# Output stage, roots and last attention sums of a hybrid attention and state-space layer, on one core

## The chip, the cores and the metric

One Trainium2 chip, one of its cores. The metric is the device time of one execution in microseconds (us), the median of several runs. One further execution was profiled; all rows below come from that one. Engines: PE is TensorE (PEld its weight loads), DVE is VectorE, ACT is ScalarE, POOL is GpSimd, SP is SyncE, whose queue issues nearly all DMAs.

## The reference, cut to what matters

One layer over 2176 tokens (128 of a prompt, 2048 latent ones), width 1024. `h = rms_norm(x) * scale + shift` is projected; one half of the result feeds differential attention (8 heads, two softmax maps each), the other a bidirectional state-space scan. Both halves are normalised, gated and projected back:

```python
a   = softmax(q1 k1) - lam * softmax(q2 k2);  att = a @ v          # per head
att = rms_norm(att, subln_g) * (1 - lam_init) * silu(g_att)
y   = rms_norm((y_f + y_b + D_skip * xs) * silu(z), ssd_norm_g)
out = concatenate([att, y]) @ w_out
y_out = rms_norm(x + gate * out, final_g)
# rms_norm(x, g) = x * rsqrt(mean(x*x) + 1e-6) * g
```

## The kernel before

The tokens are cut into 17 chunks of 128, the prompt being chunk 0. Every float32 operand of the large matmuls is split into a high part (a copy rounded by ACT) and a low part (the difference, by DVE), and each product is three matmuls: high by high, high by low, low by high.

**Order.** The program is not written in the order in which it is issued. Every operation is recorded first with its engine, a cost from a small table of formulas (`price`, line 289) and its dependences, buffer reuse included. A backward pass (`latest`, line 345) gives each operation a due time, with TensorE's work kept in program order; then a list scheduler (`simulate`, line 366) lets each engine take, among what is ready by these costs, the operation with the earliest due time. That gives one fixed order for each engine and for SP's queue; on the chip each engine runs its order and waits where an input is late. All instructions are emitted by one helper, so the profile gives line 232 for nearly all of them, and they are told apart by the names of their tiles.

**Stages.** Projections and the scan fill the first 1500 us. From about 1475 to 1550 us lie the last projection units, the inputs of the first two output chunks (`load_y`, line 1305, called for chunks 0 and 1 at line 1362 with a pool of its own, `pey`, whose ring `yr` has three buffers) and the prompt's small attention. Attention over the latent tokens follows (about 1557 to 2806 us): 128 units (8 heads, 16 query chunks), two units to a pair. For unit i, `frame(i)` (line 1583) scores six groups of 768 keys, three for each of two softmax maps, into PSUM (`ps_s`); DVE copies each out (tile `S`) with its running maximum; `s_max` (1490) takes the maximum of three; `s_exp` (1495) exponentiates a whole map of 2304 keys on ACT; `combine` (1500) forms the first map minus lambda times the second on POOL; `t_high` (1511) transposes the result on TensorE (`ps_t`), two frames later in program order, and ACT and DVE make its high and low parts (`aH`, `aL`); `av` multiplies by the values (`ps_o`). Sums of squares over each pair's output are one small matmul (`ps_q`, in `av_ssq`, 1563), whose row goes to memory and comes back in `rms_rows` (1670), with a transpose (`ps_r`), a root and a reciprocal, to be broadcast in `load_a`.

**Output stage** (about 2787 us to the end). For each chunk c, 96 matmuls of 512 columns: eight blocks of `w_out` for the y half first, then eight for the attention half. Chunks 0 and 1 run their y half together while attention drains. `load_y(c + 1)` is issued half-way through chunk c: three loads (`ya` from `y_d`, `yx` from `xbc_d`, `yz` from `z_d`), elementwise work in place in the single buffer `ya`, a sum of squares (`ysq`, `ysm`), a matmul that sums it over partitions (`ps_n`), root and reciprocal, and the parts `yH`, `yL`, which have two buffers each. `load_a(c)` (1685) does the same for the attention half with the single buffers `raw`, `rb`, `ga`, `a0`, `a1`. `finish_out` (1748) applies gate, residual and the last norm and stores. The weights `w_out` pass through the ring `yr` of pool `p3a` (three buffers, then used by `load_y`) and, for the last eight, through the ring `o` (three buffers). PSUM for output chunks comes from two pools: `psF0`, opened when the scores are done, and `psF1`, opened when attention's `psT` and `psO` close.

Of the kernel before, what the change touches and what calls it, by code (L numbers as in the profile page):

```python
# [9 lines left out]
F32 = mybir.dt.float32  # L10
# [19 lines left out]
EPS = 1e-6  # L30
TINY = 1e-37
# [10 lines left out]
B_YR, B_O = 3, 3  # L42
# [400 lines left out]
def body(tc, I, O):  # L443
# [30 lines left out]
    eps_t = cp.tile([P, 1], F32, name="eps_t")  # L474
    nc.vector.memset(eps_t, EPS)
    prm = cp.tile([P, R_END], F32, name="prm")
# [828 lines left out]
    def load_y(c, pool, ring, pn):  # L1305
# [15 lines left out]
        nc.vector.tensor_reduce(out=sm, in_=sq.rearrange("p f t -> p t f"), axis=AX.X, op=ALU.add)  # L1321
# [4 lines left out]
        nc.vector.tensor_tensor(out=y, in0=y, in1=sm.unsqueeze(1).to_broadcast([P, KT, P]), op=ALU.mult)  # L1326
        yH = p3e.tile([P, KT, P], F32R, tag="yH", name="yH", bufs=2)
        yL = p3e.tile([P, KT, P], F32R, tag="yL", name="yL", bufs=2)
        nc.scalar.copy(out=yH, in_=y)
        nc.vector.tensor_tensor(out=yL, in0=y, in1=yH.bitcast(F32), op=ALU.subtract)  # L1330
# [232 lines left out]
    def av_ssq(p):  # L1563
        pr = PR.pop(p)
        ps = psT.tile([P, 512], F32, tag="T", name="ps_q")
# [104 lines left out]
    def rms_rows(c0, c1):  # L1670
# [4 lines left out]
        ps = psT.tile([P, 512], F32, tag="T", name="ps_r")  # L1675
# [166 lines left out]
```

## Time and profile before

| | |
|---|---|
| median of 3 runs | 3195.61 us (3192.19 to 3200.39) |
| the profiled execution, own time | 3202.35 us |
| its span, first to last instruction | 3200.6 us |
| mean granted TensorE clock | 0.994 |
| busy: PE, DVE, ACT, POOL | 98%, 73%, 60%, 41% of the span |

The profiled execution is 6.74 us above the median; 1.75 us of its time lie around the span. Matmuls are pipelined and their ends are modelled, so where PE is shown as busy throughout it may still lose tenths of a microsecond: there the waits of PEld, the weight loads that precede each matmul, are read too. In a row of a timeline the bracket gives the idle time of the engine before the instruction and what ended it.

### The profile page before, as it was taken

The page shows a single profiled execution, that of the slowest core. Times are in us where ns is not written, and L with a number is a line of the kernel's source. Part 1 is how long each engine was busy: PE and PEld are TensorE (multiplying, and loading weights), DVE is VectorE, ACT ScalarE, POOL GpSimd, SP SyncE. Part 2 cuts the span into 40 slices and gives each one's busy share as a digit, 9 for nine tenths or more (in the row PEclk, how much of TensorE's full clock was granted, in tenths as well). Part 3 has the DMA queues.
Part 4 walks back from the last instruction along what each step waited for, and adds up shares of the span by engine and source line. Part 5 has one row for each costly group of instructions (what it writes and reads, how often), then busy time and mean ns, then how long its engine had stood idle before and what let it go on. Part 6 is the DMA issues. An engine that isn't in the chain of part 4 may idle for free. (4 is left out here: it accounts for less than half of the span.)

```text
span 3200.6 us, 55106 instructions
## 1 busy us (share of the span) xinstructions
PE 3136.2 (98%) x19875; PEld 2932.6 (92%) x19875; DVE 2321.5 (73%) x4701; ACT 1907.6 (60%) x3461; POOL 1302.4 (41%) x1120
## 2 busy tenths in 40 slices
PE   8999999999999999999999999999999999999999
PEld 5999999988899999998999999999999999977877
DVE  5544524766665776654599999999999999977775
ACT  4233322333466677663578878888888788864442
POOL 1011000000021122120399999999999999900000
PEclk9999999999999999999999999999999999999999
DMA  8632422867678777878413131313222211296663
GB/s 282 216 113 98 134 81 93 252 185 224 201 224 248 210 212 211 216 188 210 114 34 95 34 97 37 93 40 89 59 75 64 64 51 54 76 282 191 176 189 102
DMA packets 490722, 449.21 MB, mean 140 GB/s; under 512 B 34991, under 2 KB 437704, under 8 KB 490450
## 3 DMA queue, kind: packets, MB, share of 16 engines
q1 hardware_dynamic: 488530, 445.52, 47.6%
q8 instruction: 158, 2.59, 0.3%
q14 instruction: 114, 0.93, 0.1%
q10 hardware_dynamic: 1920, 0.17, 0.0%
HBM read 305.96 MB, written 139.62 MB: 139 GB/s over the span
## 5 line engine op out<-in xcount | busy, mean ns | idle before, releaser
L232 DVE TENSOR_SCALAR_CACHE_REDUCE S<-ps_s 128x768 f32<-128x768 f32 x768 | 716.8, 951 | 17.3 <-PE ps_s L232 11.3
L232 POOL TENSOR_TENSOR S<-S,S 128x768 f32<-128x768 f32 x384 | 710.0, 1866 | 10.1
L232 PE MATMUL ps_p<-hH,wH 128*128 128x384 f32 (+1 forms) x2112 | 698.6, 331 | 0.0
L232 PE MATMUL ps_p<-hL,wH 128*128 128x384 f32 (+1 forms) x2112 | 692.3, 328 | 0.0
L232 PE MATMUL ps_p<-hH,wL 128*128 128x384 f32 (+1 forms) x2112 | 690.9, 327 | 0.0
L232 PE MATMUL ps_s<-K,q 128*128 128x384 f32 x3072 | 678.1, 345 | 0.2
L232 ACT ACTIVATE S<-S,mx 128x2304 f32<-128x2304 f32 x256 | 569.2, 2224 | 82.3 <-DVE mx L232 82.2
L232 PEld LDWEIGHTS ps_s<-K,q 128*128 128x128 f32 x3072 | 504.5, 189 | 3.4 <-DVE S L232 1.1
L232 PE MATMUL ps_o<-aH,V 128*128 128x256 f32 x2304 | 506.4, 295 | 0.1
L232 POOL TENSOR_SCALAR_AFFINE_SELECT ar<-ar 128x512 f32<-128x512 f32 x136 | 115.7, 857 | 786.4 <-ACT ea L232 646.8
L232 DVE TENSOR_TENSOR aL<-ps_t,aH 128x384 fp32r<-128x384 f32 x768 | 406.5, 552 | 40.2 <-ACT aH L232 31.7
L232 ACT CAST aH<-ps_t 128x384 fp32r<-128x384 f32 x768 | 344.3, 478 | 122.2 <-PE ps_t L232 120.7
L232 PEld LDWEIGHTS ps_p<-hL,wH 128*128 128x128 f32 x2112 | 399.3, 189 | 1.7 <-issue 1.4
L232 PEld LDWEIGHTS ps_p<-hH,wH 128*128 128x128 f32 x2112 | 399.4, 189 | 0.9 <-issue 0.5
L232 PEld LDWEIGHTS ps_p<-hH,wL 128*128 128x128 f32 x2112 | 398.8, 189 | 1.3 <-issue 1.2
L232 POOL TENSOR_SCALAR S<-S,sm 128x768 f32<-128x768 f32 x384 | 349.3, 919 | 99.7 <-DVE sm L232 45.5
L232 PEld LDWEIGHTS ps_o<-aH,V 128*128 128x128 f32 x2304 | 382.0, 189 | 0.7 <-ACT aH L232 0.5
L232 PE MATMUL ps_t<-cst,S 128*128 128x128 f32 x2304 | 380.1, 275 | 0.2
L232 PEld LDWEIGHTS ps_t<-cst,S 128*128 128x128 f32 x2304 | 285.4, 140 | 50.4 <-POOL S L232 16.2
L232 PE MATMUL ps_o<-aL,V 128*128 128x256 f32 x1152 | 330.0, 286 | 0.0
L232 DVE TENSOR_TENSOR wL<-wr,wH 128x1024 fp32r<-128x1024 f32 x88 | 108.7, 1235 | 199.6 <-ACT wH L232 196.9
L232 PEld LDWEIGHTS ps_o<-aL,V 128*128 128x128 f32 x1152 | 218.8, 190 | 0.1
(245 smaller groups left out, 4882.1 us busy)
## 6 DMA issues: line engine op xcount, KB each, us to landing
wr<-in_w_in SPq DMA_DIRECT2D x88, 512.0 KB
ar<-row_d SPq DMA_DIRECT2D x68, 512.0 KB
q<-qH_d SPq DMA_DIRECT2D x128, 128.0 KB
q<-qL_d SPq DMA_DIRECT2D x128, 128.0 KB
xb<-xbc_d SPq DMA_DIRECT2D x17, 640.0 KB
K<-kH_d SPq DMA_DIRECT2D x48, 192.0 KB
K<-kL_d SPq DMA_DIRECT2D x48, 192.0 KB
V<-vH_d SPq DMA_DIRECT2D x24, 384.0 KB
```

Source lines behind the costliest of these rows:

```text
L232: getattr(e, name)(*[rl(v) for v in args], **{k: rl(v) for k, v in kw.items()})
```

## The change

In `load_y` the load from `y_d` goes straight into the buffer of `yL` (two buffers); the running product moves into the buffer of `yx`, the squares into that of `yz`, and `yL` is overwritten by the low part at the end. The tile `ya` and the third use of the ring per chunk are gone, and the ring of `p3a` grows from three buffers to four; the call for chunks 0 and 1 keeps its ring of three. `load_a` does the same with `a1`, which gets two buffers, and multiplies by the gate before the broadcast row instead of after. In `scale_x`, `rms_rows` and `finish_out` the root (ACT) and reciprocal (DVE) become a power of -0.5 on POOL; the scale by 1/1024 moves into the square. In `load_y` root and reciprocal stay. `s_max` takes both maps' maxima with one instruction instead of two. The last pair's `av_ssq` and the last `rms_rows` come after chunk 0's and 1's y halves in program order, with PSUM from `psF1`.

```diff
-B_YR, B_O = 3, 3
+B_YR, B_O = 4, 3
...
     def scale_x(half, b, junk):
...
-            nc.scalar.activation(out=junk, in_=xt, func=AF.Square, accum_out=st[:, 0:1])
-            nc.scalar.activation(out=st[:, 1:2], in_=st[:, 0:1], func=AF.Sqrt, scale=1.0 / D, bias=eps_t)
-            nc.vector.reciprocal(out=st[:, 0:1], in_=st[:, 1:2])
+            nc.scalar.activation(out=junk, in_=xt, func=AF.Square, scale=SCALE, accum_out=st[:, 0:1])
+            nc.gpsimd.tensor_scalar(out=st[:, 1:2], in0=st[:, 0:1], scalar1=EPS, scalar2=0.0, op0=ALU.add, op1=ALU.add)
+            nc.gpsimd.tensor_tensor(out=st[:, 0:1], in0=st[:, 1:2], in1=root, op=ALU.pow)
...
-        y = pool.tile([P, KT, P], F32, name="ya")
+        yH = p3e.tile([P, KT, P], F32R, tag="yH", name="yH", bufs=2)
+        yL = p3e.tile([P, KT, P], F32R, tag="yL", name="yL", bufs=2)
         xr, zr = (pool.tile([P, KT, P], F32, tag="yr", name=n, bufs=ring) for n in ("yx", "yz"))
-        load(out=y, in_=fpt(y_d[:, :, ts]))
+        load(out=yL.bitcast(F32), in_=fpt(y_d[:, :, ts]))
...
-        nc.vector.tensor_tensor(out=y, in0=y, in1=xr, op=ALU.add)
+        nc.vector.tensor_tensor(out=xr, in0=yL.bitcast(F32), in1=xr, op=ALU.add)
         nc.scalar.activation(out=zr, in_=zr, func=AF.Silu)
-        nc.vector.tensor_tensor(out=y, in0=y, in1=zr, op=ALU.mult)
-        sq = pool.tile([P, KT, P], F32, tag="yr", name="ysq", bufs=ring)
-        nc.scalar.activation(out=sq, in_=y, func=AF.Square)
+        nc.vector.tensor_tensor(out=xr, in0=xr, in1=zr, op=ALU.mult)
+        nc.scalar.activation(out=zr, in_=xr, func=AF.Square)
...
     def s_max(i):
         u = U[i]
-        for m in range(2):
-            nc.vector.tensor_reduce(out=u.mx[:, m, 3:4], in_=u.mx[:, m, 0:NG], axis=AX.X, op=ALU.max, negate=True)
+        nc.vector.tensor_reduce(out=u.mx[:, :, 3], in_=u.mx[:, :, 0:NG], axis=AX.X, op=ALU.max, negate=True)
...
-        nc.scalar.activation(out=rr[:n], in_=rr[:n], func=AF.Sqrt)
-        nc.vector.reciprocal(out=rr[:n], in_=rr[:n])
+        nc.gpsimd.tensor_tensor(out=rr[:n], in0=rr[:n], in1=root[:n].to_broadcast([n, P]), op=ALU.pow)
...
-        raw = p3c.tile([P, KT, P], F32, tag="raw", name="raw")
-        load(out=raw, in_=att_d[:, :, ts].rearrange("f p t -> p f t"))
+        aL = p3c.tile([P, KT, P], F32R, tag="a1", name="a1", bufs=2)
+        load(out=aL.bitcast(F32), in_=att_d[:, :, ts].rearrange("f p t -> p f t"))
...
-        nc.vector.tensor_tensor(out=rb, in0=rb, in1=ga, op=ALU.mult)
-        nc.vector.tensor_tensor(out=raw, in0=raw, in1=rb, op=ALU.mult)
+        nc.vector.tensor_tensor(out=ga, in0=aL.bitcast(F32), in1=ga, op=ALU.mult)
+        nc.vector.tensor_tensor(out=rb, in0=ga, in1=rb, op=ALU.mult)
...
-    av_ssq(NU // 2 - 1)
-    rms_rows(13, NCH)
     p2.close()
...
-        nc.vector.tensor_tensor(out=st[:, 2:3], in0=st[:, 0:1], in1=st[:, 1:2], op=ALU.add)
-        nc.scalar.activation(out=st[:, 3:4], in_=st[:, 2:3], func=AF.Sqrt, scale=1.0 / D, bias=eps_t)
-        nc.vector.reciprocal(out=st[:, 2:3], in_=st[:, 3:4])
+        nc.vector.scalar_tensor_tensor(out=st[:, 3:4], in0=st[:, 0:1], scalar=EPS, in1=st[:, 1:2],
+                                       op0=ALU.add, op1=ALU.add)
+        nc.gpsimd.tensor_tensor(out=st[:, 2:3], in0=st[:, 3:4], in1=root, op=ALU.pow)
...
         for c in range(2):
             for q in range(2):
                 mms(c, kt, q)
+    av_ssq(NU // 2 - 1, psF[1].tile([P, 512], F32, tag="F", name="ps_q"))
+    rms_rows(13, NCH, psF[1].tile([P, 512], F32, tag="F", name="ps_r"))
```

## Rows read from the trace of the kernel before

**Rows 1.** The page: busy time, share of the span and instructions of each engine.

```profile
PE 3136.2 (98%) x19875; PEld 2932.6 (92%) x19875; DVE 2321.5 (73%) x4701; ACT 1907.6 (60%) x3461; POOL 1302.4 (41%) x1120
```

**Rows 2.** Stages: length; busy PE, PEld, DVE, ACT, POOL; PE clock, DMA share, GB/s.

```profile
1500.00:1520.00 20.00, 12.54 (x64) 12.13 (x62) 10.02 (x11) 5.52 (x9) 2.32 (x2) 0.74 1.16 242
1640.00:2750.00 1110.00, 1110.00 (x8062) 1062.02 (x8061) 1036.90 (x2552) 898.55 (x1451) 1031.88 (x813) 1.00 0.23 64
...
2800.00:2860.00 60.00, 53.78 (x235) 42.90 (x235) 47.63 (x50) 36.01 (x47) 2.74 (x3) 0.91 0.99 304
2860.00:3193.00 333.00, 325.24 (x1430) 264.89 (x1428) 225.43 (x254) 142.23 (x189) 0.00 (x0) 1.00 0.58 170
```

**Rows 3.** Waits of PE over the span: total us, times, longest us.

```profile
PE ps_cb L232 <- DVE ysm L232: 7.9, 2, 7.5
PE ps_n L232 <- DVE ysm L232: 5.7, 5, 2.1
...
PE ps_q L232 <- POOL sqs L232: 2.6, 1, 2.6
```

**Rows 4.** Waits of PEld from 1640 to 2780 us.

```profile
PEld ps_t L232 <- POOL S L232: 15.2, 61, 0.3
PEld ps_t L232 <- DVE aL L232: 13.9, 58, 0.3
```

**Rows 5.** The tile ya from 2860 to 3193 us: its loads, ns, first and last.

```profile
L232 SPq DMA_DIRECT2D ya<-y_d x13: 370/377/378, 2874.0 to 3148.0; - x13
```

**Rows 6.** Timeline, 1490 to 1518 us, of DVE, SP and PE: start, length (us).

```profile
1491.02 1.22 DVE L232 TENSOR_TENSOR yx<-yx,dsk 128x1024 f32<-128x1024 f32 x1 [5.49 <-DMA yx<-xbc_d]
...
1496.06 1.23 DVE L232 TENSOR_TENSOR yL<-ya,yH 128x1024 fp32r<-128x1024 f32 x1 [1.69 <-ACT yH L232]
...
1497.97 0.48 SPq L232 DMA_DIRECT2D ya<-y_d  x1
...
1506.32 1.23 DVE L232 TENSOR_TENSOR ya<-ya,yx 128x1024 f32<-128x1024 f32 x1 [5.51 <-DMA ya<-y_d]
...
1511.92 0.80 PE L232 MATMUL ps_cb<-ysm,cst 128*128 128x128 f32 x2 [7.46 <-DVE ysm L232]
1512.37 0.67 PE L232 MATMUL ps_p<-hH,wH 128*128 128x384 f32 x1
...
1517.31 0.71 PE L232 MATMUL ps_tr<-cst,Sp 128*128 128x128 f32 x4
```

**Rows 7.** Timeline of PE in the output stage's beginning.

```profile
2831.21 0.86 PE L232 MATMUL ps_f<-woH,a 128*128 128x512 f32 x2 [2.33 <-ACT woH L232]
```

**Rows 8.** Timeline of POOL and PE at the start.

```profile
32.70 1.14 POOL L232 TENSOR_SCALAR xt<-xt,st 128x1024 f32<-128x1024 f32 x1 [31.86 <-DVE st L232]
...
40.09 0.48 PE L232 MATMUL ps_tr<-cst,xt 128*128 128x128 f32 x1 [3.46 <-DVE htmp L232]
```

**Rows 9.** Timeline of ACT at the end, and two groups of small POOL instructions.

```profile
3195.55 0.29 ACT L232 ACTIVATE st<-st,eps_t 128x1 f32<-128x1 f32 x1 [0.23 <-DVE st L232]
...
L232 POOL COPY halo<-craw 128x2 f32<-128x2 f32 x12 | 9.8, 818 | 182.5 <-ACT craw L232 182.4
...
L232 POOL MEMSET craw<- 128x1 f32 x36 | 2.8, 99 | 49.8 <-DVE cacc L232 34.0 <-PE ps_y L232 11.8 <-DVE st L232 3.8
```

**Rows 10.** Groups of instructions by form, 1700 to 2750 us: the maxima.

```profile
L232 DVE TENSOR_REDUCE mx<-mx 128x1 f32<-128x3 f32 x219 | 33.1, 151 | 3.8
```

**Rows 11.** Timeline of one attention unit, 2207 to 2215 us, on ACT, POOL and PE.

```profile
2207.37 2.23 ACT L232 ACTIVATE S<-S,mx 128x2304 f32<-128x2304 f32 x1 [1.21 <-DVE mx L232]
...
2210.32 2.23 ACT L232 ACTIVATE S<-S,mx 128x2304 f32<-128x2304 f32 x1
2210.36 1.79 POOL L232 TENSOR_SCALAR S<-S,sm 128x768 f32<-128x768 f32 x2 [0.36 <-DVE sm L232]
...
2212.12 3.68 POOL L232 TENSOR_TENSOR S<-S,S 128x768 f32<-128x768 f32 x2
...
2214.57 0.49 PE L232 MATMUL ps_t<-cst,S 128*128 128x128 f32 x3
```

More of the change, by code (lines that the diff above doesn't have):

```diff
@@ L30 @@
 EPS = 1e-6
+SCALE = D ** -0.5
 TINY = 1e-37
@@ L473, in body @@
     ident, triu, tril, ones = (cst[:, i * P:(i + 1) * P] for i in range(4))
-    eps_t = cp.tile([P, 1], F32, name="eps_t")
+    scl = cp.tile([P, 2], F32, name="scl")
+    eps_t, root = scl[:, 0:1], scl[:, 1:2]
     nc.vector.memset(eps_t, EPS)
+    nc.vector.memset(root, -0.5)
     prm = cp.tile([P, R_END], F32, name="prm")
@@ L1314, in load_y @@
         load(out=zr, in_=fpt(z_d[:, :, ts]))
-        nc.vector.tensor_tensor(out=y, in0=y, in1=xr, op=ALU.add)
+        nc.vector.tensor_tensor(out=xr, in0=yL.bitcast(F32), in1=xr, op=ALU.add)
         nc.scalar.activation(out=zr, in_=zr, func=AF.Silu)
-        nc.vector.tensor_tensor(out=y, in0=y, in1=zr, op=ALU.mult)
-        sq = pool.tile([P, KT, P], F32, tag="yr", name="ysq", bufs=ring)
-        nc.scalar.activation(out=sq, in_=y, func=AF.Square)
+        nc.vector.tensor_tensor(out=xr, in0=xr, in1=zr, op=ALU.mult)
+        nc.scalar.activation(out=zr, in_=xr, func=AF.Square)
         sm = pool.tile([P, P], F32, tag="ysm", name="ysm")
-        nc.vector.tensor_reduce(out=sm, in_=sq.rearrange("p f t -> p t f"), axis=AX.X, op=ALU.add)
+        nc.vector.tensor_reduce(out=sm, in_=zr.rearrange("p f t -> p t f"), axis=AX.X, op=ALU.add)
         pn = pn()
@@ L1325, in load_y @@
         nc.vector.reciprocal(out=sm, in_=sm)
[L1326 to L1330, printed above, removed]
+        nc.vector.tensor_tensor(out=xr, in0=xr, in1=sm.unsqueeze(1).to_broadcast([P, KT, P]), op=ALU.mult)
+        nc.scalar.copy(out=yH, in_=xr)
+        nc.vector.tensor_tensor(out=yL, in0=xr, in1=yH.bitcast(F32), op=ALU.subtract)
         cats[c, 1, 0], cats[c, 1, 1] = yH, yL
@@ L1561, in av_out, with av_ssq @@
         store(out=att_d[pr.h, :, pr.t:pr.t + 256], in_=rw)
-    def av_ssq(p):
+    def av_ssq(p, ps=None):
         pr = PR.pop(p)
-        ps = psT.tile([P, 512], F32, tag="T", name="ps_q")
+        ps = ps or psT.tile([P, 512], F32, tag="T", name="ps_q")
         mm(ps[0:1, :256], lhsT=one_r[:, 0:1], rhs=pr.sq, start=True, stop=True)
@@ L1668, in body, with rms_rows @@
     ahead = {kt: raw_wo(kt, p3a, "yr", B_YR) for kt in KORD[NPRE:NPRE + 3]}
-    def rms_rows(c0, c1):
+    def rms_rows(c0, c1, ps=None):
         n = (c1 - c0) * NH
@@ L1674, in rms_rows @@
         nc.vector.scalar_tensor_tensor(out=lv, in0=lv, scalar=EPS, in1=lv, op0=ALU.mult, op1=ALU.mult)
-        ps = psT.tile([P, 512], F32, tag="T", name="ps_r")
+        ps = ps or psT.tile([P, 512], F32, tag="T", name="ps_r")
         nc.tensor.transpose(ps[:n, :P], lv, ident)
@@ L1693, in load_a @@
         nc.scalar.activation(out=ga, in_=ga, func=AF.Silu)
-        nc.vector.tensor_tensor(out=rb, in0=rb, in1=ga, op=ALU.mult)
-        nc.vector.tensor_tensor(out=raw, in0=raw, in1=rb, op=ALU.mult)
+        nc.vector.tensor_tensor(out=ga, in0=aL.bitcast(F32), in1=ga, op=ALU.mult)
+        nc.vector.tensor_tensor(out=rb, in0=ga, in1=rb, op=ALU.mult)
         aH = p3c.tile([P, KT, P], F32R, tag="a0", name="a0")
-        aL = p3c.tile([P, KT, P], F32R, tag="a1", name="a1")
-        nc.scalar.copy(out=aH, in_=raw)
-        nc.vector.tensor_tensor(out=aL, in0=raw, in1=aH.bitcast(F32), op=ALU.subtract)
+        nc.scalar.copy(out=aH, in_=rb)
+        nc.vector.tensor_tensor(out=aL, in0=rb, in1=aH.bitcast(F32), op=ALU.subtract)
         cats[c, 0, 0], cats[c, 0, 1] = aH, aL
@@ L1755, in finish_out @@
             nc.vector.tensor_tensor(out=o[:, qs], in0=o[:, qs], in1=xr[:, qs], op=ALU.add)
-            nc.scalar.activation(out=xr[:, qs], in_=o[:, qs], func=AF.Square, accum_out=st[:, q:q + 1])
-        nc.vector.tensor_tensor(out=st[:, 2:3], in0=st[:, 0:1], in1=st[:, 1:2], op=ALU.add)
-        nc.scalar.activation(out=st[:, 3:4], in_=st[:, 2:3], func=AF.Sqrt, scale=1.0 / D, bias=eps_t)
-        nc.vector.reciprocal(out=st[:, 2:3], in_=st[:, 3:4])
+            nc.scalar.activation(out=xr[:, qs], in_=o[:, qs], func=AF.Square, scale=SCALE, accum_out=st[:, q:q + 1])
+        nc.vector.scalar_tensor_tensor(out=st[:, 3:4], in0=st[:, 0:1], scalar=EPS, in1=st[:, 1:2],
+                                       op0=ALU.add, op1=ALU.add)
+        nc.gpsimd.tensor_tensor(out=st[:, 2:3], in0=st[:, 3:4], in1=root, op=ALU.pow)
         dst = O["y_prompt"][0] if c == 0 else O["y_sample"][0, (c - 1) * P:c * P, :]
```

## The prediction

> **What bounds the kernel now.** I read the page's busy times first: PE is busy for 98% of the span, the next engine, DVE, for 73% [rows 1]. A part that is not PE's can only give back what PE loses to waiting, so the next views are the stages and PE's own waits. The reader is to see in the stages where PE falls short of the stretch and with what beside it [rows 2]: 7.5 us in the 20 us from 1500 on, none (by the records) in attention, 6.2 us in the first 60 us of the output stage, 7.8 us in the 333 us after it. The waits then name the releaser: the sums of `load_y` twice (`ps_cb` for chunks 0 and 1, `ps_n` later) and the last pair's squares (`ps_q`) [rows 3]. In attention PE's records overlap, so the weight loads' waits are read: 29.1 us in 1140 us, half on POOL's result, half on DVE's low part [rows 4]. All that the change touches therefore has some 21 us of plain PE idle time and 29 us of small waits to win from; the rest is matmul.
>
> **The steady output chunks (gain 6.5 us).** A chunk is 96 matmuls. The single buffer `ya` is loaded, worked on to its low part, and only then loaded again: 13 loads start between 2874.0 and 3148.0 us, one every 22.8 us [rows 5]. PE waits 5.7 us for the sums [rows 3] and is idle for 333.00 - 325.24 = 7.76 us in that stretch [rows 2], so the ring, slightly longer than PE's own chunk, is what ends last. Afterwards the load goes to a `yL` buffer that was last read in the y half of the chunk before the current one, `yx` and `yz` have two buffers each, and the three loads no longer stand in the ring. DVE, ACT and POOL are busy for 225, 142 and 0 of the 333 us, DMA for 58%, so PE is next. `load_a` gains a buffer too, but PE doesn't name `a` among its large waits: nothing for it. The whole 7.76 us is the most; I take 6.5, because some waits of the fixed order always remain, and 3 as the least.
>
> **The inputs of chunk 1 (gain 5 us).** The largest single stall is here: PE waits 7.46 us for chunk 1's sums, because `ya` of chunk 1 was issued only at 1497.97, after chunk 0's low part, and landed 8.3 us later, and the 15 matmuls behind the stall take 1517.31 - 1512.37 = 4.94 us at half clock, 2.5 us more than at full [rows 6]. The stretch's granted clock is 0.74 [rows 2]; in these matmuls it is the lower level, after PE had stood idle. With the change `yL` has its second buffer at once. But this pool keeps a ring of three, each chunk now uses two, and the first of them holds the product until chunk 0's low part is written: chunk 1's `yz` takes that very buffer, so it is now `yz` that is issued after 1497. What improves is that chunk 1's `yx` has a free buffer, so that DVE isn't held for 5.49 us in front of chunk 0's reciprocal and product [rows 6]; chunk 0's low part, and with it the late load, comes up to 5.5 us sooner, against some 1 us more behind the load (a table load and SiLU in the place of one addition). So 4.5 us of the stall go, and perhaps part of the slow clock: 5 us taken, between 9.9 (7.46 + 2.5, nothing left) and a loss of 1. The Trainium skill, ScalarE: Activation LUTs, section What ACT_TABLE_LOAD costs, puts a switch of tables at 2.66 us with its drain; by it the loss would be about 2.4 us and not 1.
>
> **The beginning of the output stage (0).** `av_ssq` and the last `rms_rows`, with their copy, their store, their load and the store of the roots, are moved past 96 matmuls of PE and past the loads of `w_out` on SP's queue. PE's wait of 2.6 us for `ps_q` [rows 3] goes. But the following wait, 2.33 us at 2831.21, is for a block of `w_out` [rows 7], and from 2800 to 2860 DMA is busy for 99% [rows 2]: PE would come earlier to the same late load. So nothing is taken. Above: the four-buffer ring starts one block sooner and all 6.2 us of idle time go. Below: chunk 2's `y` can no longer be loaded early (its buffer is chunk 0's `yL` until PE is through that y half), and it and two other loads of 512 KB, at 304 GB/s 1.7 us each, may stand in front of weights: 5 us lost. The roots of chunks 13 to 16 come later, and their readers are ten chunks away.
>
> **The roots (0).** In `scale_x` a table load, a root and a reciprocal go and two POOL instructions come. The first scaled tile was ready at 33.84 and PE waited until 40.09 for the modulation, not for it [rows 8]; these 6 us are the cover, and without it the price would be the POOL instructions. In `finish_out` the power is on the path only once, after the last matmul, in the place of 0.29 us on ACT and a reciprocal. No power is in the trace; the nearest small POOL instructions take 0.10 and 0.82 us [rows 9], so the end moves by -0.4 to +0.4 us; I take 0. POOL is empty from 2860 to 3193 [rows 2]. In `rms_rows` two powers are queued on POOL while it still combines the last units; at a few tenths to 2 us each they delay the last transposes, while PE has the y halves of chunks 0 and 1 to do.
>
> **One maximum for two maps (0, and the widest bounds).** 128 maxima of 151 ns go from DVE [rows 10]. What comes is a dependence: the first map's exponential can start only after the second map is scored. Now it starts before, and behind the unit's last maximum lies one exponential: it starts at 2207.37, POOL's combination at 2210.36, its first sum ends at 2212.12 + 3.68/2 = 2213.96, and PE takes the first transposes at 2214.57, 0.6 us later [rows 11]. The exponential at 2210.32 is the next unit's first one. Afterwards the two behind the last maximum belong to one unit, so the sum comes one exponential and its accumulator read, some 2.4 us, later: 1.8 us past the slack. If PE's order stayed as it is, each unit would lose this; since the distance from a unit's scores to its transposes contains one earlier stall too, about half, 0.9 us, or 115 us in 128 units. It will not stay: the scheduler prices an exponential at 2.2 us and puts other work of PE in front, of which there is enough (the next unit's scores, an older pair's products, four units of buffers), and latency then costs nothing. I take 0, with -29 (all waits of [rows 4] gone) and +115 as ends.
>
> **Sum.** 6.5 + 5 + 0 + 0 + 0 = 11.5 us off 3202.35, the profiled execution: 3190.9. That execution is 6.74 us over the median, so the median forecast is 3184.
>
> **Rivals.**
> Slower through the merged maximum. The scheduler moves the transposes exactly to where its prices say that POOL is done, and they then have no slack; the read of the accumulator, which follows each exponential and which it prices too low, comes twice in the chain. 0.2 us per exponential, 0.4 a unit, of which 0.3 stay: 38 us in 128 units, 3222. For it: 0.6 us of slack against 2.4. Against it: each other hop in the chain is priced too high. It decides as soon as the transposes wait for POOL by more than 0.1 us a unit above today's 0.12 (15.2 us in 1140), about one unit each 9.6 us.
>
> Faster through the merged maximum. DVE is busy for 1037 of 1110 us in attention [rows 2], and with 0.15 us less a unit and a new order half of the 29 us of small waits go: 3184 - 15 = 3169. The Trainium skill points this way: VectorE: DVE Perf Modes, section Rules for kernel authors, says to reduce the number of chained operations. Against it: PE has the larger share.
>
> No gain, though the edits do what they say: chunk 1's `yz` takes the place of `ya` in the same stall, and in the output stage DMA or DVE's fixed order holds PE where the ring did: 3195.
>
> **How the numbers follow.** Forecast 0.45, slower rival 0.22, faster rival 0.15, no gain 0.18. The forecast's own terms leave 3174 to 3196. 0.3%, 9.6 us, is about what a measurement of this kernel can tell from no change: faster means under 3186, slower over 3205. The forecast gives 0.27 faster and 0.18 the same, the faster rival 0.14 and 0.01, no gain 0.02, 0.14 and 0.02 slower, the slower rival 0.03 the same and 0.19 slower: 0.43, 0.36, 0.21. The range 3164 to 3222 leaves out half of each outer rival, some 0.18.
>
> **What would show it.** In the changed profile: PE's wait for `ps_n` under 2 us in all and idle time under 2 us from 2860 to the end; the stall on `ps_cb` under 4 us, released by work on `yz`; the same or later arrival of the last block of `w_out`; PEld's waits in attention as now, about 29 us, with POOL's combination 2 to 3 us further behind the scores. The prediction is wrong if those waits move by more than 15 us either way, if POOL's power takes more than a few microseconds, or if the new loads push the weights back by more than 5 us.

## The result and the profile after

| | before | after |
|---|---|---|
| median, us (runs) | 3197.0 (4) | 3286.4 (4) |
| lowest to highest, us | 3192.2 to 3200.4 | 3281.3 to 3287.8 |
| profiled span, us | 3200.6 | 3283.4 |

The changed kernel is slower: ratio 1.0278, 95% interval 1.0260 to 1.0296, some 89 us. The forecast was 3184, its range 3164 to 3222. In the experiments a ratio is to executions of the kernel before on the same chip, with its 95% interval behind it. The runs were taken on several chips, so a small difference between two of them is better read from their ratios.

The page's busy times of the changed kernel, against [rows 1]: DVE and ACT have less to do, POOL more, and PE's share fell.

```profile
PE 3179.9 (97%) x19875; PEld 2949.2 (90%) x19875; DVE 2293.2 (70%) x4537; ACT 1869.7 (57%) x3407; POOL 1388.8 (42%) x1174
```

The stages of the changed kernel (columns as in [rows 2]), cut where PE's waits are:

```profile
1500.00:1520.00 20.00, 14.47 (x78) 13.87 (x77) 7.71 (x11) 7.85 (x11) 2.33 (x2) 0.83 1.14 237
1640.00:2750.00 1110.00, 1108.95 (x7814) 1040.07 (x7813) 984.40 (x2363) 863.92 (x1408) 999.12 (x789) 1.00 0.22 62
2812.00:2876.00 64.00, 31.45 (x157) 25.55 (x156) 20.71 (x31) 20.40 (x33) 61.47 (x17) 0.73 0.25 86
...
2892.00:2943.00 51.00, 28.36 (x107) 20.51 (x106) 26.15 (x23) 16.84 (x17) 20.72 (x1) 0.80 0.59 176
2943.00:3276.00 333.00, 331.39 (x1464) 271.57 (x1462) 230.56 (x253) 132.43 (x176) 8.81 (x16) 1.00 0.63 181
```

Three things are to be seen. In the last stretch PE is idle for 1.61 us of 333 where it was 7.76 [rows 2]: the input ring is gone, as forecast. In attention PE does 7814 matmuls in 1110 us where it did 8062 [rows 2], though it is busy all the time by the records. And two stretches around the end of attention, 64 and 51 us long, in which PE works half of the time at a granted clock of 0.73 and 0.80, have no counterpart before.

For attention the tile of the scores gives the length, in the kernel before and in the changed one (min/median/max ns, first and last start):

```profile
L232 PE MATMUL ps_s<-K,q x3072: 331/336/446, 1552.0 to 2777.8; 128*128 128x384 f32 x192
```

```profile
L233 PE MATMUL ps_s<-K,q x3072: 331/337/459, 1547.9 to 2812.4; 128*128 128x384 f32 x192
```

From the first score to the last it was 1225.8 us and is 1264.5: 38.7 us more, 0.30 for each of 128 units. The waits of the weight loads from 1640 to 2780 us say the same, against [rows 4]: 56.0 us in place of 29.1, every unit and not every second one waits for POOL's sum, and the scores and the pairs' sums wait too.

```profile
PEld ps_t L233 <- POOL S L233: 30.5, 116, 0.3
PEld ps_s L233 <- DVE S L233: 14.8, 58, 0.3
PEld ps_q L233 <- POOL sqs L233: 10.7, 58, 0.2
```

PE's waits from 2780 us to the end (total us, times, longest), against [rows 3]:

```profile
PE ps_n L233 <- DVE ysm L233: 18.0, 1, 18.0
PE ps_q L233 <- POOL sqs L233: 15.3, 1, 15.3
PE ps_t L233 <- POOL S L233: 14.2, 3, 12.6
```

POOL's timeline names what stands in front (start, length in us):

```profile
2822.59 1.84 POOL L233 TENSOR_TENSOR S<-S,S 128x768 f32<-128x768 f32 x1
2824.36 21.76 POOL L233 TENSOR_TENSOR rr<-rr,scl 8x128 f32<-8x128 f32 x1
2846.12 0.90 POOL L233 TENSOR_SCALAR S<-S,sm 128x768 f32<-128x768 f32 x1
...
2851.22 21.72 POOL L233 TENSOR_TENSOR rr<-rr,scl 96x128 f32<-96x128 f32 x1
2873.02 0.72 POOL L233 TENSOR_TENSOR sqs<-sq,sqs 64x256 fp32r<-64x256 f32 x1
...
2907.50 20.72 POOL L233 TENSOR_TENSOR rr<-rr,scl 32x128 f32<-32x128 f32 x1 [20.03 <-DVE rr L233]
```

The three powers of `rms_rows` take 21.8, 21.7 and 20.7 us. The first stands between two parts of the last unit's combination, the second in the middle of the squares of the last pair but one. The scheduler had no reason to keep them out of the way: its `price` takes a power for any two-input instruction on POOL, 128 x 2.1 + 150 ns = 0.42 us. PE, whose order is fixed, waits behind them:

```profile
2848.84 1.54 PE L233 MATMUL ps_t<-cst,S 128*128 128x128 f32 x6 [12.62 <-POOL S L233]
...
2873.79 0.37 PE L233 MATMUL ps_q<-sqs,one_r 128*1 128x256 f32 x1 [15.34 <-POOL sqs L233]
```

The third holds no unit, but its rows `rr` lie in the buffer `ysm`, which `load_y` needs next. DVE's reduction waits until the roots have been stored, and PE with it:

```profile
2929.76 1.87 DVE L233 TENSOR_REDUCE ysm<-yz 128x128 f32<-128x1024 f32 x1 [18.39 <-DMA rs_d<-rr]
```

So the theory before the experiments: the merged maximum costs 38 us in attention, the three powers some 50 us after it, and the rest of the change is a small gain. A difference of a few us between two traces is not to be trusted by itself: the two profiled executions of the kernel before lie 7 and 8 us above its median.

### The profile page after: what moved, and what is told of

The parts are those of the page before. It is cut to its first block, busy times and chain, and to the rows that moved or that the text cites. A ratio compares the mean times of both kernels' runs of the same rounds, so it can differ in the third digit from the quotient of the medians.

```text
span 3283.4 us, 54651 instructions
## 1 busy us (share of the span) xinstructions
PE 3179.9 (97%) x19875; PEld 2949.2 (90%) x19875; DVE 2293.2 (70%) x4537; ACT 1869.7 (57%) x3407; POOL 1388.8 (42%) x1174
## 5 line engine op out<-in xcount | busy, mean ns | idle before, releaser
L233 PE MATMUL ps_s<-K,q 128*128 128x384 f32 x3072 | 696.3, 349 | 1.7 <-DVE S L233 0.4
L233 ACT CAST aH<-ps_t 128x384 fp32r<-128x384 f32 x768 | 335.1, 483 | 141.0 <-PE ps_t L233 139.5
L233 PE MATMUL ps_t<-cst,S 128*128 128x128 f32 x2304 | 364.5, 278 | 14.7 <-POOL S L233 14.2
L233 PEld LDWEIGHTS ps_t<-cst,S 128*128 128x128 f32 x2304 | 264.8, 141 | 61.8 <-POOL S L233 48.2
```

The lines of the kernel that those rows point to most:

```text
L233: getattr(e, name)(*[rl(v) for v in args], **{k: rl(v) for k, v in kw.items()})
```

## The experiments

**The causes apart.** In the first run the root of `rms_rows` is back on ACT and DVE.

```diff
-        nc.gpsimd.tensor_tensor(out=rr[:n], in0=rr[:n], in1=root[:n].to_broadcast([n, P]), op=ALU.pow)
+        nc.scalar.activation(out=rr[:n], in_=rr[:n], func=AF.Sqrt)
+        nc.vector.reciprocal(out=rr[:n], in_=rr[:n])
```

> The changed kernel with the root of rms_rows back on ACT and DVE (square root, then reciprocal); nothing is left out. Theory (two causes: the merged maximum costs 39 us in attention, the powers of 21.7 us on POOL cost about 55 us around the output stage): 3286 - 55 to 60, so 3226 to 3232, with the last scores to the last transposes near 24 us and not 62. Rival (the 62 us there come from the late products of the last units and from av_ssq's new place, not from POOL's queue): the stretch stays near 62 us and the time within 10 us of 3286.

Measured: 3233.2 us, ratio 1.0118 (1.0104 to 1.0132); from the last scores (2813.5) to the last transposes (2840.6) 27.1 us, where the changed kernel has 62.2. Both are a little above what the theory said (3226 to 3232, 24); the rival falls.

The second has two maxima again in the changed kernel.

```diff
-        nc.vector.tensor_reduce(out=u.mx[:, :, 3], in_=u.mx[:, :, 0:NG], axis=AX.X, op=ALU.max, negate=True)
+        for m in range(2):
+            nc.vector.tensor_reduce(out=u.mx[:, m, 3:4], in_=u.mx[:, m, 0:NG], axis=AX.X, op=ALU.max, negate=True)
```

> The changed kernel with the maximum of the two maps back as two instructions; nothing is left out. Theory: first to last scores go from 1264.5 back to about 1226 us, the time to about 3286 - 39 = 3247, and the stall of some 38 us behind POOL's powers stays. Rival (the loss in attention comes from the double-buffered inputs or the order around them, not from the maximum): first to last scores stay near 1264 us and the time near 3286.

Measured: 3245.5 us, ratio 1.0154 (1.0138 to 1.0169); scores 1544.9 to 2773.1, 1228.2 us. The theory holds. PE's waits after attention in this run:

```profile
PE ps_n L233 <- DVE ysm L233: 17.8, 1, 17.8
PE ps_q L233 <- POOL sqs L233: 17.8, 1, 17.8
PE ps_t L233 <- POOL S L233: 13.7, 1, 13.7
```

The third has both edits.

> The changed kernel with both undone (two maxima, rms_rows' root on ACT and DVE); the inputs, the roots of the scaled tiles and of the last rows, and the late av_ssq stay; nothing is left out. Theory: what is left is the gain of the two input terms, 4 us at chunk 1 and 6 us in the steady chunks, less 0 to 3 us at the beginning of the output stage: 7 to 10 us below the kernel before, ratio 0.9970 to 0.9978. Rival (the late av_ssq and the late last roots give the gain back at the beginning of the output stage): ratio 0.999 to 1.001. Rival (the two causes don't add, each covers part of the other): more than 10 us above the kernel before.

Measured: 3195.0 us, ratio 0.9993 (0.9984 to 1.0003). The causes add: the maximum is 3233.2 - 3195.0 = 38.2 us, the powers 3245.5 - 3195.0 = 50.5, of which the three waits above are 49.3; together 88.7. From this kernel to the changed one it is 3286.4 - 3195.0 = 91.4; by the ratios, the two causes are 1.25% and 1.61% and both together 2.85%. But the 7 to 10 us expected below the kernel before are not there: the rival that the gain is given back fits. Its stages show the gain itself, against [rows 2]:

```profile
1500.00:1520.00 20.00, 16.30 (x90) 15.69 (x89) 9.02 (x12) 7.82 (x10) 2.33 (x2) 0.87 1.13 234
...
2860.00:3187.00 327.00, 325.21 (x1434) 266.21 (x1432) 221.05 (x242) 125.04 (x168) 9.68 (x16) 1.00 0.60 174
```

The fourth is the kernel before with the merged maximum alone (the second edit reversed).

> The kernel before with the merged maximum alone; nothing is left out. Theory (the merged maximum makes the whole loss in attention by itself): 3197 + 39 = 3236, first to last scores 1264 us, the transposes' wait for POOL's combination twice as long (15 to 30 us in 1640 to 2780). Rival (it costs only together with the other edits, which shift the order): below 3206. Rival (faster by a saved instruction): below 3190.

Measured: 3241.8 us, ratio 1.0143 (1.0127 to 1.0158), scores 1552.0 to 2816.7 (1264.7 us), the transposes' wait for POOL 31.2 us in 114 units. The maximum makes the loss alone. It is some 6 us above the 3236 expected; in the trace these lie behind the last scores (429.1 us to the end, 422.8 in the kernel before), and why is open.

**Why the merged maximum costs.** Here two reductions stay, so that only the dependence is new.

```diff
-        for m in range(2):
-            nc.vector.tensor_reduce(out=u.mx[:, m, 3:4], in_=u.mx[:, m, 0:NG], axis=AX.X, op=ALU.max, negate=True)
+        nc.vector.tensor_reduce(out=u.mx[:, 0, 3:4], in_=u.mx[:, 0, 0:NG], axis=AX.X, op=ALU.max, negate=True)
+        nc.vector.tensor_reduce(out=u.mx[:, :, 3], in_=u.mx[:, :, 0:NG], axis=AX.X, op=ALU.max, negate=True)
```

> The kernel before with two reductions kept for each unit: the first over the first map, the second over both maps, so that the first exponential comes behind both maps' scores as with the merged maximum, and no DVE instruction is saved. Nothing is left out. Theory (the dependence, one exponential and its accumulator read more between a unit's scores and its sum, is what costs): as the merged maximum or more, first to last scores 1260 to 1275 us, time 3232 to 3250. Rival (the merged instruction's form or the order that the scheduler finds with one instruction less costs): first to last scores near 1226 us, time below 3205.

Measured: 3236.2 us, ratio 1.0139 (1.0117 to 1.0160), scores 1264.4 us. The dependence costs; the instruction's form does not.

The next tests the slower rival's reason, with the merged maximum in the kernel before.

```diff
-            return n * 0.833 * 1.0 + (52 if psum else 94) + extra + (93 if "accum_out" in a else 0)
+            return n * 0.833 * 1.0 + (52 if psum else 94) + extra + (281 if "accum_out" in a else 0)
```

> The kernel before with the merged maximum, and with the scheduler's price for an exponential's accumulator read raised from 93 to 281 ns. Nothing is left out. Theory (the slower rival's reason: the scheduler puts the transposes where its too low price says that POOL is done): with the right price it puts more in front, the transposes' wait for POOL falls below 20 us in 1640 to 2780, the time falls from 3242 to 3200 to 3215. Rival (the loss is in the order that the dependence forces, or the other prices matter more): 3230 to 3250, the waits stay near 30 us. Third: the new price alone disturbs the order, above 3250.

Measured: 3256.8 us, ratio 1.0197 (1.0181 to 1.0212), scores 1290.1 us. The waits of the weight loads, 1640 to 2780 us:

```profile
PEld ps_s L232 <- DVE S L232: 59.8, 113, 0.9
PEld ps_t L232 <- POOL S L232: 12.2, 56, 0.3
```

The transposes wait less for POOL, as the theory said, but the scores now wait for DVE to empty their bank: the wait moved and grew. The third case came, above 3250. Raising this one price does not give the loss back. Whether the new price also costs in a kernel with two maxima was not run, so the price is not ruled out as a part of the cause; it is only not borne out.

To hold the order fixed, the next run takes the schedule of the two separate maxima and emits the merged one in the second's place, with the first map's exponential directly ahead of the second's.

```diff
             for i in order:
+                if i in self.held:
+                    continue
                 ops[i].emit()
+                if i in held:
+                    ops[held[i]].emit()
...
+                nc.ops[-1].emit = lambda: tc.nc.vector.tensor_reduce(out=u.mx[:, :, 3].real(), in_=u.mx[:, :, 0:NG].real(),
+                                                                     axis=AX.X, op=ALU.max, negate=True)
```

> The kernel before with the merged maximum, but in the order that the scheduler finds for the two separate ones: PE's and POOL's orders are those of before row by row, DVE's lacks only the first map's maximum, and on ACT the first map's exponential comes right before the second map's. Nothing is left out. Theory A (the latency costs, and the scheduler's new order saved part of it; so the prediction argued): the transposes wait for POOL 1 us and more a unit, 3290 or more. Theory B (the new order costs, the latency is covered by the units in flight): within 15 us of before, 3190 to 3212. Between them, 3230 to 3250: the new order is worth nothing either way.

Measured: 3437.0 us, ratio 1.0750 (1.0733 to 1.0766). Scores run from 1550.4 to 3013.5, so that a unit takes (1463.1 - 1225.8) / 128 = 1.85 us more. Theory A holds in size, but not by its wait: for POOL the weight loads of the transposes wait 26.7 us in all, 0.3 at a time. The groups of DVE and POOL from 1640 to 2750 us (count | busy us, mean ns | idle us before them and who ended it):

```profile
L233 DVE RECIPROCAL sm<-sm 128x1 f32<-128x1 f32 x97 | 15.9, 164 | 233.9 <-ACT S L233 233.9
...
L233 POOL TENSOR_SCALAR S<-S,sm 128x768 f32<-128x768 f32 x290 | 261.4, 911 | 236.2 <-DVE sm L233 236.2
```

The same DVE group in the kernel before:

```profile
L232 DVE RECIPROCAL sm<-sm 128x1 f32<-128x1 f32 x116 | 19.0, 164 | 22.5 <-ACT S L232 22.5
```

DVE reaches the reciprocal and stands there 233.9 / 97 = 2.4 us a unit for the second exponential, where it stood 0.2. Behind it in DVE's order are the low parts `aL`, which free the transposes' bank, and PE's largest wait from 1640 to 2780 us is for them:

```profile
PE ps_t L233 <- DVE aL L233: 130.5, 99, 1.9
```

In that run the two exponentials hold ACT's copies for 4.4 us, which could be the whole price. So the next puts one copy between them, PE's and POOL's orders as before.

```diff
+                out[k:k + 2] = [e, nx, e + 1]
```

> As the run with the merged maximum in before's order, but on ACT the next high-part copy stands between the two exponentials of a unit, so that they hold the copies no longer than before. PE's and POOL's orders are those of before. Nothing is left out. Theory A (the later sum costs by itself): still above 3290, the waits now name POOL's sum. Theory A' (only the two exponentials in a row cost): below 3240.

Measured: 3502.3 us, ratio 1.0940 (1.0921 to 1.0959); DVE stands 264.3 us in 93 units, 2.8 each, in front of the same reciprocal. The later exponential costs by itself, 2.34 us a unit in this order ((1525.4 - 1225.8) / 128); theory A' falls. Theory A's wait did not come here either: the weight loads of the transposes wait 24.2 us for POOL's sum.

Does a ring through POOL set the period? The two small instructions on a pair's squares go to DVE, first with the merged maximum in the kernel before.

```diff
-        nc.gpsimd.tensor_tensor(out=sq[:, 0], in0=sq[:, 0], in1=sq[:, 1], op=ALU.add)
+        nc.vector.tensor_tensor(out=sq[:, 0], in0=sq[:, 0], in1=sq[:, 1], op=ALU.add)
-        nc.gpsimd.tensor_tensor(out=pr.sq[64:128], in0=sq[:, 0], in1=pr.sq[0:64].bitcast(F32), op=ALU.subtract)
+        nc.vector.tensor_tensor(out=pr.sq[64:128], in0=sq[:, 0], in1=pr.sq[0:64].bitcast(F32), op=ALU.subtract)
```

> The kernel before with the merged maximum, and with the two small instructions on the pairs' squares (0.74 us each) moved from POOL to DVE. Nothing is left out. Theory (a ring through POOL sets the unit's period: POOL has 8.95 us of work a unit and stands idle 0.9 us for the later sum): with 0.74 us less on POOL the period falls from 9.88 to 9.6 or less, first to last scores 1200 to 1230 us, time 3175 to 3205. Rival (POOL's load doesn't matter, only the latency of the chain does): first to last scores 1255 us or more, time above 3230.

Measured: 3262.7 us, ratio 1.0209 (1.0188 to 1.0230), scores 1283.5 us. The theory falls. The rival's numbers came, but the run doesn't single it out, since the largest wait of the weight loads is a new one:

```profile
PEld ps_o L232 <- ACT aH L232: 47.7, 57, 0.9
```

The same move with two maxima (on the kernel with both undone):

> The kernel with both undone, with the same two instructions moved from POOL to DVE. Nothing is left out. Theory (POOL's queue is what the transposes wait for, 15 us in 1640 to 2780): those waits fall below 8 us, time 3175 to 3190, a version below both kernels. Rival (DVE, busy for 93%, takes the place): waits on DVE's low part grow by as much, 3190 to 3215.

Measured: 3224.0 us, ratio 1.0080 (1.0062 to 1.0097), scores 1250.5 us. Both forecasts were missed. There is no new dependence, the wait for POOL fell to 5.5 us from 15.7 as the theory said, and still attention takes 22 us more than in the run's base. The rival was nearer, but the waits that grew are not those for the low part (0.8 us, 14.1 in the base): the scores wait 22.2 us for DVE. On DVE the additions took 977 ns each (57 of them, some 740 on POOL), and DVE is busy for 1065 us of 1110. Less work on POOL is worth nothing here if DVE takes it.

**The powers.** In the kernel with both undone, the last `rms_rows` alone uses the power.

```diff
+        if c0 == 13:
+            nc.gpsimd.tensor_tensor(out=rr[:n], in0=rr[:n], in1=root[:n].to_broadcast([n, P]), op=ALU.pow)
```

> Both maxima as before, and POOL's power in the last rms_rows alone (the others by ACT and DVE); its rows share the buffer of the sums of the y input. Nothing is left out. Theory: 18 to 20 us over the kernel with both undone (3195), 3213 to 3215, with one wait of PE for the sums of about 18 us near 2850. Rival (the power's 20.7 us are hidden when POOL is not held up before): below 3200.

Measured: 3212.0 us, ratio 1.0049 (1.0032 to 1.0066), 17.0 us over its base, with one wait of 17.8 us for `ysm`. The theory holds, a little below its sum. Then the rows get a buffer of their own:

```diff
-        rr = p3a.tile([P, P], F32, tag="ysm", name="rr")
+        rr = cst[:, P:2 * P] if c0 == 13 else p3a.tile([P, P], F32, tag="ysm", name="rr")
```

> As the kernel with the power in the last rms_rows alone, but with these rows in a buffer of their own, so that no load of the y input's sums waits for the power. Nothing is left out. Theory (the 18 us wait is for the shared buffer): 3193 to 3199, no wait of PE for the sums above 2 us. Rival (the roots themselves are needed early, or the power holds another engine up): 3208 or more.

Measured: 3198.9 us, ratio 1.0008 (0.9999 to 1.0018); no wait for the sums. 13 of the 17 us were the shared buffer. The other 4 can be followed in the timeline: the small root of an output row stands behind the power on POOL, DVE behind that root, and PE waits 8.85 us for `yH`, which comes behind DVE's work (2.96 us in the run's base).

```profile
2849.75 20.75 POOL L233 TENSOR_TENSOR cst<-cst,scl 32x128 f32<-32x128 f32 x1 [38.35 <-DVE cst L233]
...
2870.48 0.54 POOL L233 TENSOR_TENSOR st<-st,scl 128x1 f32<-128x1 f32 x1
2871.05 1.41 DVE L233 SCALAR_TENSOR_TENSOR o<-o,st,fg 128x512 f32<-128x512 f32 x2 [15.35 <-POOL st L233]
...
2878.46 0.79 PE L233 MATMUL ps_f<-woH,yH 128*128 128x512 f32 x1 [8.85 <-ACT yH L233]
```

The price by size:

```diff
+            for s, e in ((0, 16), (16, 48), (48, P)):
+                nc.gpsimd.tensor_tensor(out=rr[:n, s:e], in0=rr[:n, s:e], in1=root[:n].to_broadcast([n, e - s]), op=ALU.pow)
```

> As the kernel with the power in the last rms_rows alone and in rows of their own, but the power of 32 x 128 is issued as three instructions of 16, 32 and 80 columns. Nothing is left out. Theory (0.17 us a column and next to no fixed cost): 2.7, 5.4 and 13.5 us, together about as one. Rival (a fixed cost for each instruction, or one that grows with partitions): other ratios than 1 : 2 : 5, or a sum above 23 us.

Measured, by POOL's groups:

```profile
L233 POOL TENSOR_TENSOR cst<-cst,scl 32x80 f32<-32x80 f32 x1 | 13.1, 13096 | 0.0
L233 POOL TENSOR_TENSOR cst<-cst,scl 32x32 f32<-32x32 f32 x1 | 5.4, 5420 | 0.0
L233 POOL TENSOR_TENSOR cst<-cst,scl 32x16 f32<-32x16 f32 x1 | 2.9, 2917 | 38.1 <-DVE cst L233 38.1
```

(13096 - 2917) / 64 = 159 ns a column, and 2917 - 16 x 159 = 0.4 us fixed: the theory holds. In the changed kernel 8, 32 and 96 partitions took 21.8, 20.7 and 21.7 us, so the time does not grow with the partitions.

**What is left of the gain.** The kernel before once more:

> The kernel before once more, for a second trace. Nothing is changed. The kernel with both undone was 6 us shorter than the kernel before by the two profiles, and 0.7 us by the medians. Theory (the profiled execution of before was a long one, and what varies lies in the output stage, where its input ring is just longer than PE's chunk): here PE's idle time from 2860 to the end is 2 to 5 us and not 7.8. Rival (what varies lies before attention, in the loads): idle time there 7 to 8 us again, and the first scores start at another time than 1552.

Measured: 3196.0 us. From 2860 to 3193 us PE was busy for 324.92, idle for 8.08: the 7.76 of [rows 2] repeat, so the short idle time that the theory expected did not come. That doesn't settle it, since the profiled execution was a long one again, 3204.0 us where the median is 3196.0: no trace shows an execution of this kernel near its median. PE's stall for chunk 1's sums was 6.4 us, PE busy there 13.60 of 20. So the gain of the steady chunks stands against two traces, and something gives most of it back. The late sums are the first suspect: they go back ahead of the 96 matmuls.

```diff
+    av_ssq(NU // 2 - 1)
+    rms_rows(13, NCH)
     p2.close()
```

> The kernel with both undone (two maxima, rms_rows' root on ACT and DVE), and with av_ssq and the last rms_rows back in front of the 96 matmuls. What is left of the change: double-buffered inputs, roots of the scaled tiles and of the last rows by POOL's power. Nothing is left out. Theory (the late sums give back what they save, since PE meets the same loads of w_out): as the kernel with both undone, 0.9985 to 1.0000. Rival (they cost some 3 us at chunk 2's late y input): 0.997 to 0.998. Rival (they gain their 2.6 us wait): 1.000 to 1.001.

Measured: 3193.7 us, ratio 0.9982 (0.9973 to 0.9991): 5.8 us below the kernel before, and the first run that is. The rival fits, that the late sums cost some 3 us: (0.9993 - 0.9982) x 3197 = 3.5, though the intervals meet. The traces agree: with the late sums PE starts the output stage's rest 3.6 us earlier (last scores 2776.8 against 2780.4) and has as much left at 2860 (1434 matmuls against 1431), because it waits 2.96 us for chunk 2's `yH`, whose input is loaded later. From the last scores to the end it is 417.7 us with the late sums and 413.4 without, against 422.8 and 423.1 in the two traces of the kernel before. A ring of four for the loads of chunks 0 and 1, first with the late sums, then without:

```diff
-        load_y(c, pey, 3, lambda: bank("cb"))
+        load_y(c, pey, 4, lambda: bank("cb"))
```

> The kernel with both undone (two maxima, rms_rows' root on ACT and DVE), and with a ring of four instead of three buffers for the loads of chunks 0 and 1, so that chunk 1's z input need not wait until chunk 0's low part is written. Nothing is left out. Theory (what is left of the stall at 1512 is that late load): PE is busy for 18 us or more of 1500 to 1520, first scores 1 to 3 us earlier, ratio to before 0.998. Rival (nothing is left there, or the load only moves into the 116% of DMA traffic there): as with three, 0.9993 to 1.0003.

> What is left of the change when the merged maximum, rms_rows' power and the late sums are undone, with a ring of four for the loads of chunks 0 and 1. Nothing is left out. Theory (the stall of chunk 1 is the late z input): 1 to 3 us below the same with a ring of three, ratio to before 0.9972 to 0.998. Rival (nothing left there): 0.998 to 0.999.

Measured: 3195.3 us, ratio 0.9993 (0.9984 to 1.0002), and 3194.4 us, ratio 0.9981 (0.9972 to 0.9990), both as with a ring of three. PE is busy for 16.86 and 16.48 us of the 20. What the theory took for the rest of the stall is something else. In the kernel before PE waited 0.49 us for chunk 0's sums and 7.46 for chunk 1's [rows 6]:

```profile
1485.68 0.46 PE L232 MATMUL ps_cb<-ysm,cst 128*128 128x128 f32 x2 [0.49 <-DVE ysm L232]
```

In the changed kernel, with a ring of three, the one wait that is left for these sums is chunk 0's. Chunk 1's are not waited for at all: PE's order has other matmuls in front of them, and among these are two waits for the prompt's attention. The first is the late z input by another way: ACT stands 6.03 us for it and makes the copy `ap` afterwards.

```profile
1489.42 0.46 PE L233 MATMUL ps_cb<-ysm,cst 128*128 128x128 f32 x2 [1.84 <-DVE ysm L233]
...
1501.42 0.53 SPq L233 DMA_DIRECT2D yz<-z_d  x1
...
1507.23 1.28 ACT L233 ACT_TABLE_LOAD   x1 [6.03 <-DMA yz<-z_d]
1508.53 1.06 ACT L233 ACTIVATE yz<-yz 128x1024 f32<-128x1024 f32 x1
...
1511.84 0.57 ACT L233 CAST ap<-ps_tr 128x512 fp32r<-128x512 f32 x1
...
1512.46 0.33 PE L233 MATMUL ps_y<-ap,vp 128*128 128x128 f32 x1 [3.31 <-ACT ap L233]
...
1515.29 0.69 PE L233 MATMUL ps_y<-kp,qp 128*128 128x128 f32 x2 [2.22 <-DMA qp<-qL_d]
1515.78 0.73 PE L233 MATMUL ps_cb<-ysm,cst 128*128 128x128 f32 x2
```

With a ring of four the sums of chunk 1 reach PE at 1497.00 us and the wait for `ap` is gone, but PE then waits 2.0 us for `rwp` and 1.6 for `Sp`. From the scan's last matmul on `bz` to the first scores it waits 6.3 us in all, in the kernel with both undone as in the one with a ring of four. Then the scaled tiles' roots go back to ACT and DVE as well:

```diff
-            nc.gpsimd.tensor_scalar(out=st[:, 1:2], in0=st[:, 0:1], scalar1=EPS, scalar2=0.0, op0=ALU.add, op1=ALU.add)
-            nc.gpsimd.tensor_tensor(out=st[:, 0:1], in0=st[:, 1:2], in1=root, op=ALU.pow)
+            nc.scalar.activation(out=st[:, 1:2], in_=st[:, 0:1], func=AF.Sqrt, scale=1.0 / D, bias=eps_t)
+            nc.vector.reciprocal(out=st[:, 0:1], in_=st[:, 1:2])
```

> What is left of the change when the merged maximum, rms_rows' power and the late sums are undone, and also the scaled tiles' roots are back on ACT and DVE: the double-buffered inputs and the last rows' root by POOL's power remain. Nothing is left out. Theory (the two POOL instructions ahead of each scaled tile cost some 4 us in the first 630 us): the first matmul of the scan on bz at 874 to 878 us, 3 to 4 us below the same with those roots on POOL, ratio to before 0.9965 to 0.9975. Rival (the later start is order or chance): 879 to 881 us, ratio 0.998 to 0.999.

Measured: 3185.7 us where the kernel before took 3192.0 on the same chip, ratio 0.9983 (0.9974 to 0.9992). The scan's first matmul on `bz` starts at 874.3 us, as the theory said; over all traces it starts at 875.6 on the mean with these roots on ACT and DVE (nine, 873.6 to 878.3) and at 879.8 with them on POOL (eleven, 877.2 to 881.7). PE's wait for the scaled tiles from 140 to 630 us is as in the kernel before, 0.4 us. That wait in the changed kernel, and in this one:

```profile
PE ps_tr L233 <- POOL xt L233: 2.7, 2, 2.1
```

```profile
PE ps_tr L233 <- POOL xt L233: 0.4, 2, 0.2
```

The time does not follow: the ratio is that of the rival. That these roots delay the scan by some 4 us is shown, though the waits above are only half of it; that the whole program is longer for it is not, and 4 us are no more than these intervals can tell. For the kernel with both undone the stretches add up to what was measured, by means over the traces for the first two and by its own trace for the others: the scan starts 4 us later, the way from its last matmul on `bz` to the first scores is 3 us shorter, attention is 2 us longer (1228.1 us for 1225.8 and 1226.3, and 1227.9 to 1229.5 in the other versions with two maxima and the squares on POOL; why was not looked for), the rest 5 us shorter: 2 us, and 2.2 by the ratio. For the last kernel the same sum gives some 12 us (412.2 us behind the last scores), and 5.4 were measured by the ratio; the difference is open. The best versions are these without the late sums, some 6 us under the kernel before and, by the ratios, some 95 under the changed one.

## Why the prediction was wrong

**The roots** (taken 0) failed most: 50.5 us. The step said that no power is in the trace and took a row of small copies and fills, 0.10 and 0.82 us [rows 9], as the nearest, then allowed "a few tenths to 2 us each" in `rms_rows`. Those rows bound the one-column power well (0.55 us, the end did not move), but a power of 128 columns was priced as if only its existence counted. It takes 0.4 + 128 x 0.159 = 20.8 us. The cover named, the y halves of chunks 0 and 1 on PE, also failed: PE's and POOL's orders are fixed, so what stands behind the power waits, whatever else there would be to do. That the scheduler had a power at 0.42 us when it put one into the last unit's combination was not seen; where it would put a power at its measured price was not tried. That `rr` shares the buffer `ysm` with the sums of `load_y` was missed as well (13 us by the runs). For the scaled tiles the step looked at the first tile alone [rows 8]; the later ones made the scan start 4 us later. The prediction's own sign of being wrong, a power of more than a few microseconds, came. The Trainium skill, GPSIMD Engine Reference, section 4.1 Engine selection, calls elementwise work with two inputs about twice as slow there as on VectorE. In this trace an addition of 768 columns on POOL takes 1.86 us, 2.4 ns a column, and the power 159 ns a column: nothing in that sentence prices a power, and no run here has one on VectorE. For the pairs' squares the trace agrees only in part: of two instructions of 0.74 us each on POOL, the subtraction took 0.42 us on DVE and the addition 0.98.

**The maximum** (taken 0, between -29 and +115) is the slower rival, in place and size: 38 us forecast, 38.2 measured (46 by the run with the maximum alone), and its sign came (the wait for POOL rose from 15.2 to 30.5 us, 0.13 a unit, over the 0.1 from which it was to decide). The step's first half was right in size: the 1.8 us past the slack that each unit would lose in the old order were 1.85, and 2.34 with a copy between the exponentials. Halving them to 0.9 was wrong, and so was "latency then costs nothing": the new order takes back 1.55 of 1.85 and leaves 0.30. The rival's reason was not borne out by the price run, so that its size was met by luck. In the old order the way was not the one argued either: the later exponential holds DVE at the reciprocal, not the transposes at POOL. In the new order both waits are there. From 1640 to 2750 us the changed kernel does some 112 units, and these hops wait once in every unit:

```profile
ACT aH L233 <- PE ps_t L233: 120.0, 112, 1.4
DVE sm L233 <- ACT S L233: 46.1, 112, 0.6
PEld ps_t L233 <- POOL S L233: 29.5, 112, 0.3
```

In the kernel before the last two waited in every second unit (58 times, 22.5 and 14.6 us). POOL waits 52.2 us for what comes of the reciprocal, and on ACT the exponentials stand behind such a copy, so the hops could close a ring: transposes, copy, exponentials, reciprocal, POOL's sum, the next transposes. That such a ring keeps the last 0.30 us a unit is argued from these waits and not tested. That the order has no slack left on any engine fits three runs, in which another price or another engine for the squares cost some 17, 21 and 28 us against their own bases, by the ratios.

**The steady chunks** (gain 6.5): 6.15 in the changed kernel (1.61 us idle for 7.76), right in the mechanism and in size, against two long executions of the kernel before.

**Chunk 1's inputs** (gain 5): the way was wrong. The step had the late load come up to 5.5 us sooner behind chunk 0's low part. It was issued 1501.42 - 1489.42 = 12.0 us behind chunk 0's sums, where it had been 1497.97 - 1485.68 = 12.3. The stall on chunk 1's sums went because PE's order puts other matmuls in front of them, and waits of 1.84, 3.31 and 2.22 us took its place. From the scan's last matmul on `bz` to the first scores it is 89.0 us on the mean of ten traces with the new inputs and a ring of three (87.8 to 90.0), and 92.0 in eight with the old ones (89.9 to 94.1): a gain of 3 us, below the 5 taken and inside the bounds, but not by the step's argument, so that it is luck in part. A switch of tables costs less than the prediction quotes for it: in the rows above its load takes 1.28 us, and the next instruction follows at once.

**The beginning of the output stage** (0, between -5 and +6.2): some 3.5 us lost by the ratios, 4.3 by the traces, by the cause named for the lower end, chunk 2's later input. Inside the bounds; the value taken was too high.

## What to carry to other kernels

An operation that the trace doesn't show has no price by its neighbours of another kind: ask what it costs for each column before putting it into a queue that others stand behind, keep its bound open until a run has shown it, and look at what price the scheduler gives it. A merged instruction is a new dependence; where the orders are fixed and PE, DVE and POOL are all over 90% busy, saving 0.15 us of work against 2.4 us of latency loses, and a new order gives back only part. A small result that lies in a buffer shared with the main path makes the path wait for it, however late it is needed.

## What was not expected of the hardware

POOL's power costs 159 ns for each column and 0.4 us fixed, the same on 8 as on 96 partitions; 34 powers of one column took 0.63 us on the mean. The addition of 64 x 256 that took 741 ns on POOL took 977 ns on DVE in one run and 1250 in the other, the subtraction behind it, of the same shape, 420 and 691 ns; why they differ was not tried. After the wait of 12.62 us six transposes of PE took 1.54 us that took 0.87 before it. The granted clock of these 1.54 us is 0.50, the lower of the two levels (1.2 and 2.4 GHz), so the stalls cost some matmuls at half speed on top.
